# Summing the attention halves without GpSimd, and loading the spatial weights on the other queue

## The chip, the cores and the metric

The kernel runs on one core of a Trainium2 chip. The metric is the device time of one execution in microseconds; the time before is 2110.33 us, the median of three runs (2108.59 to 2112.67). The engines are named as the profile names them: PE is TensorE's matmul, PEld its weight load, ACT is ScalarE, DVE is VectorE, POOL is GpSimd, SP is SyncE. All work of an engine runs in the order in which it was emitted.

## The reference, cut to what matters

The program is a two-layer encoder block on a sequence of 1024 positions with 1024 features, in float32. Each layer is `x <- x + RMSNorm(mixer(RMSNorm(x)))`.

Layer 0 is a gated MLP. Three dense projections of width 2048 give u, v and g; v is normalised and mixed along each chunk of 128 positions by a 128x128 matrix per head (16 heads), then gated and projected back:

```python
u = gelu(u); v = layer_norm(gelu(v))
sg = einsum('hpq,bcqhd->bcphd', w_s, vc) + b_s
y = u * sg * silu(g);  return y @ w_out
```

Layer 1 is attention in three groups with strides 1, 4 and 16 (half window 64 keys), 16 heads of 64 features in each group, with a relative-position bias read from a table. The three groups' outputs are merged by their softmax denominators, gated and projected back:

```python
logits = q @ k.T * dh**-0.5 + bias[rel * dilation]   # masked outside the window
p = exp(logits - max);  o = (p / den) @ v;  lse = max + log(den)
y = sum_g softmax(lse)_g * o_g;  return (y * silu(gate)) @ w_out
```

## The kernel before, in words

**Numbers in two parts.** Every matmul operand is split into a high part, which is rounded to TensorE's reduced float32 form, and a low part, which is the rest. A product of two such operands is computed as high times high, high times low and low times high. ACT writes the high part and DVE (sometimes POOL) subtracts to get the low part. A class `Pieces` does this for all dense weights: it loads pieces of 128x512 into three buffers on SP's queue (L149), ACT makes the high part (L165), DVE the low part (L167), and up to eight pieces lie ready ahead of the matmuls.

**A written-out order.** There is no automatic scheduling. A `Plan` keeps a clock that each matmul advances by its modelled time, and a heap of steps with due times. After each dense matmul it emits the steps that have come due. So a due time is a place in the order of emission; an engine reaches the step when what it got before is done. `plan.until` emits further steps until a condition on the order holds.

**Layer 0.** First v for all 2048 columns is projected and kept in `gv`. Twelve transfers `toep_fill` (L477) write the bias rows of each group 128 times over into three tensors in HBM, four heads at a time: 768 KB for group 0, 1536 KB for group 1, 512 KB for group 2. They are due 20, 50, 80, ... 350 plan units after the first part of the v projection, on SP's queue, and the results are read only in layer 1. Then 16 heads follow: `dense` computes u and g of a head, two halves of 512 positions each, in two alternating PSUM banks "D", which ACT evacuates with gelu and silu. After each head `spatial` sets the steps of its mixing among the matmuls of the next head, from `t0`, half a unit after the end of the head's projections: `ws_load` (the head's 128x128 matrix `wsr` and its bias `bsr`, 64 KB each, on SP's queue), `ws_tr` (PE transposes the matrix, ACT and DVE split it), `v_split`, `ws_sum` and four times `mix`. `ws_load` is due at t0 - 6, which is past already when it is set, so it is emitted with the next matmul, just ahead of `ws_tr` at t0.

**Layer 1.** A unit is a pair of heads (p of 8) in one group (g of 3), 24 units in all. For each, `v_load` and `v_split` bring the values and split them into `u.vs`; `dense(q_part)` and `dense(k_part)` project queries and keys; their evacuation fills two tiles for queries and two for keys, one for each head of the pair (`a`). A key tile has two halves along its free axis: the first holds the high part on all 128 partitions (ACT writes 64, POOL copies them to the other 64, L932), the second holds the low part on 64 partitions (DVE) and zeros on the other 64 (POOL, L923). The tag "ks" has three buffers, a unit takes two. Then eight `attend` steps, four for each head of the pair, are laid over the following unit's projections: `qk` (PE into bank "S"), `smax` (DVE), `ex` (ACT), `trs` (PE transposes into bank "T"), `ph` and `pl` (ACT and DVE split the probabilities), `pv` (PE into bank "O"), and `o1`, `o2`, `o3`, which put the output together.

For `pv` the stationary operand is `u.vs` with 64 columns of high and 64 columns of low values, so 64 partitions of bank "O" hold products with the high values and 64 those with the low values; the moving operand holds high and low probabilities side by side, 256 columns for each of two blocks. In groups 0 and 2 all four products are summed: `o1` (ACT) copies 64 partitions x 512 columns from the other 64 partitions to `tm`, `o2` (DVE, L273) adds the own 64 partitions x 512 columns, and `o3` (POOL, L1087) adds the two column halves into `u.o`. In group 1 three products are computed and `o2` alone finishes.

When a pair's three groups are done, `weights` merges them in four quarters of 256 positions: the quarters 0 and 2 on POOL, 1 and 3 on DVE, for the last pair all on DVE. All other transfers of layer 1 (values through HBM, merge weights, results) are on SP's queue as well.

Of the kernel before, what the change touches and what calls it, by code (L numbers as in the profile page):

```python
# [203 lines left out]
def encoder_block(ctx: ExitStack, tc: tile.TileContext, x, norm_pre, norm_post, a_w_in, a_w_s,  # L204
# [269 lines left out]
    prep.close()  # L474

    def toep_fill(g, h):
        nc.sync.dma_start(toep[g][h:h + 4],  # L477
                            vec[h:h + 4, VOFF[g]:VOFF[g] + VLEN[g]].unsqueeze(1).to_broadcast(
                                [4, P, VLEN[g]]))

# [67 lines left out]
            pc.free(2)  # L548

    done_a = set()  # L550

    def spatial(h, ug, t0, dt):
        vs, sg, T = {}, {}, {}
        hc = slice(128 * h, 128 * h + 128)

        def ws_load():
            T["w"] = sp.tile([P, P], F32, name="wsr")
            nc.sync.dma_start(T["w"], a_w_s[h])
            T["b"] = sp.tile([P, P], F32, name="bsr")
            nc.sync.dma_start(T["b"], bcast_row(a_b_s, h * P, P))  # L560

        def ws_tr():
            b = bank("T")
# [34 lines left out]
            if cc == 3:  # L598
                done_a.add(h)

        plan.at(t0 - 6, ws_load)
        plan.at(t0, ws_tr)
        plan.at(t0 + 0.3, v_split, 0)
        plan.at(t0 + 1.5, v_split, 1)
        plan.at(t0 + 2.5, ws_sum)
        for cc in range(4):
            plan.at(t0 + 4.0 + dt * cc, mix, cc)

# [47 lines left out]
    for k in range(8):  # L656
        w_rows(b_w_out, 128 * k, 0)

    for h in range(NH):
        u = sp.tile([P, S], F32, name="us")  # L660
        g = sp.tile([P, S], F32, name="gs")
        dense(lambda b, hh: act(u[:, 512 * hh:512 * hh + 512], b, AF.Gelu_apprx_tanh))
        dense(lambda b, hh: act(g[:, 512 * hh:512 * hh + 512], b, AF.Silu))
        tt(u, u, g, OP.mult)
        if h == 0:
            plan.until(lambda: not any(f is ln_apply for _, _, f, _ in plan.heap))
        spatial(h, u, plan.now + 0.5, 3.0)
# [216 lines left out]
    def v_split(u, k):  # L884
        if k == 0:
            if u.prev is not None and u.prev.prev is not None:
                plan.until(lambda: u.prev.prev.pv_left == 0)
            u.vs = b1.tile([P, 8, 2, 2, 64], F32R, name="vs2")
        src = u.vt.rearrange("p m (a d) -> p m a d", a=2)
        hi = u.vs[:, :, :, 0, :]  # L890
        if k == 0:
            act(hi, src)
            plan.after(VALUES_AT[1], v_split, u, 1)
        else:
            tt(u.vs[:, :, :, 1, :], src, hi.bitcast(F32), OP.subtract)
            u.v_there = True

    def q_part(u):
        def evac(b, hh):
            if hh == 0:  # L900
                if u.prev is not None:
                    plan.until(lambda: u.prev.qk_left[0] == 0)
                plan.until(lambda: u.v_there)
                u.q = [b1.tile([P, S], F32R, name="qs", bufs=3) for _ in range(2)]
            for a in range(2):
                r = 64 * a
                act(place(u, u.q[a], r, r + 64, hh), source(u, b, r, r + 64), scale=-0.125)
            for a in range(2):
                r = 64 * a
                hi = place(u, u.q[a], r, r + 64, hh)  # L910
                stt(place(u, u.q[a], 64 - r, 128 - r, hh), source(u, b, r, r + 64), -0.125,
                    hi.bitcast(F32), OP.mult, OP.subtract)
        return evac

    def k_part(u):
        def evac(b, hh):
            if hh == 0:
                if u.prev is not None:
                    plan.until(lambda: u.prev.qk_left[0] == 0)
                u.k = [b1.tile([P, 2, S], F32R, name="ks", bufs=3) for _ in range(2)]  # L920
                for a in range(2):
                    o = 64 - 64 * a
                    nc.gpsimd.memset(u.k[a][o:o + 64, 1].bitcast(F32), 0.0)  # L923
            for a in range(2):
                r = 64 * a
                act(place(u, u.k[a][:, 0], r, r + 64, hh), source(u, b, r, r + 64))
# [23 lines left out]
    def attend(u, a, n, t0):  # L950
# [109 lines left out]
        def o1():  # L1060
            if u.o is None:
# [5 lines left out]
            w = 256 if g == 1 else 512  # L1067
            T["m"] = pool.tile([P, 512], F32, name="tm")
            act(T["m"][rs, :w], T["o"][64 - r0:128 - r0, :w])

        def o2():
            b, m = T["o"], T["m"]
            if g == 1:
                tt(res(u.o[rs]), b[rs, :256].rearrange("p (b j) -> p b j", b=2),
                   m[rs, :256].rearrange("p (b j) -> p b j", b=2), OP.add)
                u.o_left -= 1
            else:
                tt(m[rs], b[rs], m[rs], OP.add)

        def o3():  # L1080
            if g == 0:
                m = T["m"][rs].rearrange("p (i a b t) -> p a i t b", i=2, a=2, t=8)
# [373 lines left out]
```

## Time and profile before

| | before |
|---|---|
| median of three runs | 2110.33 us |
| profiled execution, whole | 2109.72 us |
| its span, first to last instruction | 2107.9 us |
| mean granted TensorE clock, share of full speed | 0.982 |
| PE busy | 2003.0 us (95%) |
| DVE busy | 1242.0 us (59%) |
| ACT busy | 1063.0 us (50%) |
| POOL busy | 413.5 us (20%) |

The span is 1.8 us shorter than the profiled execution, and that execution is 0.6 us below the median. On the span's axis the v projection ends at about 202 us, the 16 heads' projections run to about 622 us, the first output projection to about 833 us, the attention units from about 955 us, the last pair's from about 1822 us, and the second output projection ends the program. TensorE's clock has two levels, 1.2 and 2.4 GHz; the profile gives the granted clock of a stretch as a share of the higher one.

### The profile page before, as it was taken

How to read it: one execution, taken by the hardware profiler on the slowest of the kernel's cores; microseconds unless marked ns; L12 is line 12 of the kernel's file. 1: busy time of each engine (PE TensorE's matmuls, PEld its weight loads, DVE VectorE, ACT ScalarE, POOL GpSimd, SP SyncE). 2: the span in 40 equal slices, each digit the busy share in tenths (PEclk: the TensorE clock that was granted, in tenths of full speed). 3: DMA queues.
4: the chain of work that ended last, by engine and by line, in shares of the span. 5: the costliest groups of instructions: out<-in, count | busy, mean ns of one | idle time of the engine just before them, and what ended most of it. 6: DMA issues, size and time to landing. Idle time of an engine off the chain costs nothing.

```text
span 2107.9 us, 30338 instructions
## 1 busy us (share of the span) xinstructions
PE 2003.0 (95%) x10809; PEld 1709.1 (81%) x10809; DVE 1242.0 (59%) x2742; ACT 1063.0 (50%) x2239; POOL 413.5 (20%) x480
## 2 busy tenths in 40 slices
PE   7999898989999978999999999999999999999998
PEld 5888686868888757988888988888888889787776
DVE  6223443534456798346576575675765765767647
ACT  5222232323346676256655556556656555676632
POOL 1000000000000143012151250241331512525241
PEclk9999999999999999999999999999999999999999
DMA  4222121221113455331222241331322232413277
GB/s 148 82 84 68 65 80 65 79 66 56 55 35 121 153 172 186 124 89 54 81 84 86 76 114 52 93 99 56 101 72 82 82 87 75 109 46 85 92 208 272
DMA packets 222339, 201.97 MB, mean 96 GB/s; under 512 B 17179, under 2 KB 192955, under 8 KB 222188
## 3 DMA queue, kind: packets, MB, share of 16 engines
q1 hardware_dynamic: 222188, 200.04, 31.2%
q8 instruction: 85, 1.39, 0.3%
q14 instruction: 66, 0.54, 0.1%
HBM read 171.26 MB, written 40.26 MB: 100 GB/s over the span
## 4 chain that ended last, share of the span: by engine, by line
PE 75%; DVE 11%; DMA 6%; POOL 3%; issue 3%; ACT 2%; SPq 0%; DVEq 0%; ACTq 0%; POOLq 0%
PE psD L255 56%; PE psS L255 8%; PE psO L255 6%; PE psT L255 3%; DVE wt L167 3%; PE psT L266 3%; DMA wsr<-in_a_w_s_dram 3%; DVE o L273 1%; POOL o L1087 1%; DVE qs L276 1%; DVE tm L273 1%; POOL o L273 1%; DVE xs L1006 1%; DMA y<-yd 1%; ACT wt L165 1%
## 5 line engine op out<-in xcount | busy, mean ns | idle before, releaser
L255 PE MATMUL psD<-hTh,wt 128*128 128x512 f32 x2816 | 916.2, 398 | 0.0
L255 PEld LDWEIGHTS psD<-hTh,wt 128*128 128x128 f32 x2816 | 519.3, 190 | 90.3 <-ACT gv L270 0.4
L255 PE MATMUL psD<-hTl,wt 128*128 128x512 f32 x1408 | 559.2, 397 | 0.0
L255 PE MATMUL psD<-wt,hTh 128*128 128x256 f32 (+1 forms) x1760 | 365.4, 300 | 1.3 <-DMA gv<-in_x_dram 0.6
L167 DVE TENSOR_TENSOR wt<-raw,wt 128x512 fp32r<-128x512 f32 x344 | 268.8, 803 | 163.3 <-ACT wt L165 144.6
L255 PEld LDWEIGHTS psD<-hTl,wt 128*128 128x128 f32 x1408 | 267.6, 190 | 48.2
L255 PEld LDWEIGHTS psD<-wt,hTh 128*128 128x128 f32 x1760 | 286.4, 191 | 13.7 <-POOL wt L167 1.7
L165 ACT ACTIVATE wt<-raw 128x512 fp32r<-128x512 f32 x360 | 215.5, 626 | 157.7 <-PE psD L255 104.0
L255 PE MATMUL psD<-wt,hTl 128*128 128x256 f32 (+1 forms) x880 | 263.0, 299 | 0.7 <-DVE hTl L273 0.7
L270 ACT ACTIVATE xs<-xs,st 128x256 f32<-128x256 f32 (+2 forms) x384 | 176.8, 461 | 164.3 <-DVE st L1006 163.5
L1087 POOL TENSOR_TENSOR o<-tm 64x256 f32<-64x256 f32 x128 | 127.3, 995 | 385.1 <-DVE tm L273 375.3
L255 PEld LDWEIGHTS psD<-wt,hTl 128*128 128x128 f32 x880 | 168.3, 191 | 5.8 <-DVE hTl L273 1.3
L273 DVE TENSOR_TENSOR pt<-psT,pt 128x512 fp32r<-128x512 f32 (+1 forms) x192 | 115.1, 600 | 96.4 <-ACT pt L270 94.6
L273 POOL TENSOR_TENSOR yo<-yo,gp 128x1024 f32<-128x1024 f32 x6 | 15.8, 2628 | 725.2 <-ACT yo L270 719.2
L1006 DVE CUSTOM_DVE_ANT_0 xs<-psS,bias 128x256 f32<-128x256 f32 (+1 forms) x256 | 95.9, 412 | 76.5 <-PE psS L255 74.6
L255 PEld LDWEIGHTS psO<-pt,vs 128*128 128x128 f32 (+1 forms) x640 | 99.5, 178 | 32.3 <-DVE pt L273 18.6
L255 PE MATMUL psS<-ks,qs 128*128 128x256 f32 x640 | 111.8, 289 | 11.6 <-POOL ks L932 11.6
L255 PE MATMUL psO<-pt,vs 128*128 128x256 f32 (+1 forms) x640 | 108.5, 283 | 13.6 <-DVE pt L273 13.6
L273 DVE TENSOR_TENSOR ks<-psD,ks 64x512 fp32r<-64x512 f32 x96 | 66.1, 688 | 88.2 <-ACT ks L270 86.9
L255 PEld LDWEIGHTS psS<-ks,qs 128*128 128x128 f32 x640 | 98.2, 192 | 22.6 <-POOL ks L932 13.5
L932 POOL TENSOR_SCALAR ks<-ks 64x512 fp32r<-64x512 f32 x96 | 61.7, 642 | 279.4 <-ACT ks L270 273.7
L270 ACT ACTIVATE tm<-psO 64x512 f32<-64x512 f32 (+1 forms) x192 | 100.1, 521 | 31.8 <-PE psO L255 20.4
(204 smaller groups left out, 2742.9 us busy)
## 6 DMA issues: line engine op xcount, KB each, us to landing
raw<-in_b_w_in_dram SPq DMA_DIRECT2D x160, 256.0 KB, 3.2
raw<-in_a_w_in_dram SPq DMA_DIRECT2D x96, 256.0 KB, 3.0
raw<-in_a_w_out_dram SPq DMA_DIRECT2D x96, 256.0 KB, 2.8
y<-yd SPq DMA_DIRECT2D x56, 256.0 KB, 5.8
cb<-sc SPq DMA_DIRECT2D x64, 192.0 KB, 5.2
vd<-tm SPq DMA_DIRECT2D x80, 128.0 KB, 1.8
vt<-vd SPq DMA_DIRECT2D x16, 512.0 KB, 4.8
yd<-cb SPq DMA_DIRECT2D x28, 256.0 KB, 2.5
```

The lines of the kernel that those rows point to most:

```text
L165: self.nc.scalar.activation(hi, src, AF.Copy)
L167: e.tensor_tensor(lo, src, hi.bitcast(F32), op=OP.subtract)
L255: nc.tensor.matmul(o, l, r, start=start, stop=stop)
L266: nc.tensor.transpose(o, i, ident)
L270: nc.scalar.activation(o, i, f, **k)
L273: (e or nc.vector).tensor_tensor(o, a, b, op=op)
L276: nc.vector.scalar_tensor_tensor(o, a, s, b, op0=op0, op1=op1)
L932: nc.gpsimd.tensor_scalar(place(u, u.k[a][:, 0], o, o + 64, hh), hi.bitcast(F32), 1.0, 0.0, op0=OP.mult, op1=OP.add)
L1006: nc.vector.tensor_tensor_reduce(out=o, in0=s_, in1=bi, op0=OP.add, op1=OP.min, scale=1.0, scalar=3.0e38, accum_out=col(0, t))
L1087: nc.gpsimd.tensor_tensor(o, m[:, 0], m[:, 1], op=OP.add)
```

## The change: what it does

Three things are changed. `toep_fill` and `ws_load` issue their transfers from ACT's queue instead of SP's, and `ws_load` runs earlier: heads 0 and 1 are loaded before the loop over the heads, and head h + 2 is loaded four units after the `t0` of head h (the two tiles have two buffers each). The zeros of the first key tile are set when the unit's queries are evacuated instead of its keys; those of the second stay. In groups 0 and 2 the values of the second head of a pair are stored low first, so that the partitions on which the output lies always hold the products with the high values; the output is then the sum of three products instead of four (low times low is left out): `o1` copies 256 columns instead of 512, and `o2` and `o3` are two additions on DVE of 256 columns each, both with one operand in PSUM. POOL has no part in it any more.

```diff
     def toep_fill(g, h):
-        nc.sync.dma_start(toep[g][h:h + 4],
+        nc.scalar.dma_start(toep[g][h:h + 4],
...
+    def ws_load(h):
+
+        if h < NH:
+            T = ws[h] = {}
+            T["w"] = sp.tile([P, P], F32, name="wsr")
+            nc.scalar.dma_start(T["w"], a_w_s[h])
+            T["b"] = sp.tile([P, P], F32, name="bsr")
+            nc.scalar.dma_start(T["b"], bcast_row(a_b_s, h * P, P))
...
-        plan.at(t0 - 6, ws_load)
         plan.at(t0, ws_tr)
...
+        plan.at(t0 + 4.0, ws_load, h + 2)
...
+    ws_load(0)
+    ws_load(1)
     for h in range(NH):
...
-        hi = u.vs[:, :, :, 0, :]
+        v4 = u.vs.rearrange("p m a e d -> p m (a e) d")
+        hi, lo = (v4[:, :, 0:4:2], v4[:, :, 1:4:2]) if u.g == 1 else (v4[:, :, 0:4:3], v4[:, :, 1:3])
...
+    def k_tile(a):
+
+        t = b1.tile([P, 2, S], F32R, name="ks", bufs=3)
+        nc.gpsimd.memset(t[64 - 64 * a:128 - 64 * a, 1].bitcast(F32), 0.0)
+        return t
...
                 u.q = [b1.tile([P, S], F32R, name="qs", bufs=3) for _ in range(2)]
+                u.k = [k_tile(0)]
...
-                u.k = [b1.tile([P, 2, S], F32R, name="ks", bufs=3) for _ in range(2)]
-                for a in range(2):
-                    o = 64 - 64 * a
-                    nc.gpsimd.memset(u.k[a][o:o + 64, 1].bitcast(F32), 0.0)
+                u.k.append(k_tile(1))
...
-            act(T["m"][rs, :w], T["o"][64 - r0:128 - r0, :w])
+            T["m"] = pool.tile([P, 512], F32, name="tm")[:, :256]
+            src = T["o"][64 - r0:128 - r0]
+            if g == 1:
+                act(T["m"][rs], src[:, :256])
+            else:
+                act(T["m"][rs].rearrange("p (i q) -> p i q", i=2),
+                    src.rearrange("p (i e q) -> p e i q", i=2, e=2)[:, 0])
...
-                tt(m[rs], b[rs], m[rs], OP.add)
+                m = m[rs].rearrange("p (i q) -> p i q", i=2)
+                tt(m, b[rs].rearrange("p (i e q) -> p e i q", i=2, e=2)[:, 0], m, OP.add)
...
-                m = T["m"][rs].rearrange("p (i a q) -> p a i q", i=2, a=2)
+                m = T["m"][rs].rearrange("p (i q) -> p i q", i=2)
+                b = T["o"][rs].rearrange("p (i e q) -> p e i q", i=2, e=2)[:, 1]
                 o = u.o[rs, 256 * n:256 * n + 256].rearrange("p (i q) -> p i q", i=2)
-            nc.gpsimd.tensor_tensor(o, m[:, 0], m[:, 1], op=OP.add)
+            tt(o, b, m, OP.add)
```

## Rows read from the trace of the kernel before

**Rows 1.** The page's first part: busy us, share of the span, instructions.
```profile
PE 2003.0 (95%) x10809; PEld 1709.1 (81%) x10809; DVE 1242.0 (59%) x2742; ACT 1063.0 (50%) x2239; POOL 413.5 (20%) x480
```

**Rows 2.** Windows: PE, PEld, DVE, ACT, POOL busy; granted clock; DMA; units 1 to 6.
```profile
955.00:1822.00 867.00, 846.51 (x5203) 750.57 (x5202) 554.87 (x1331) 521.80 (x1239) 247.55 (x320) 1.00 0.29 82
```

**Rows 3.** What PE waited for in the heads (200 to 640): us, times, longest.
```profile
PE psT L266 <- DMA wsr<-in_a_w_s_dram: 29.0, 3, 10.4
```

**Rows 4.** SP's transfers in time, second of three such places: start, us.
```profile
323.61 0.61 SPq L477 DMA_DIRECT2D toep<-vec  x1
324.27 6.61 SPq L558 DMA_DIRECT2D wsr<-in_a_w_s_dram  x1
```

**Rows 5.** The chain of waits at that place: start, us.
```profile
324.27 17.74 DMA wsr<-in_a_w_s_dram
```

**Rows 6.** Windows right behind the three waits, columns as in rows 2.
```profile
235.00:246.00 11.00, 11.00 (x47) 9.17 (x48) 6.30 (x12) 4.14 (x6) 0.00 (x0) 0.86 0.17 49
342.00:353.00 11.00, 10.95 (x42) 9.04 (x43) 5.33 (x10) 4.14 (x6) 0.00 (x0) 0.76 0.17 48
450.00:461.00 11.00, 10.88 (x46) 9.07 (x47) 6.22 (x12) 4.14 (x6) 0.00 (x0) 0.86 0.17 49
```

**Rows 7.** Waits of ACT in the heads, and of SP's queue over the span.
```profile
ACT us L270 <- PE psD L255: 128.2, 32, 5.8
...
SPq L149 <- DVE wt L167: 1129.1, 219, 18.0
```

**Rows 8.** Groups by form: count | busy us, mean ns | idle before.
```profile
L1087 POOL TENSOR_TENSOR o<-tm 64x256 f32<-64x256 f32 x128 | 127.3, 995 | 385.1 <-DVE tm L273 375.3 <-PE psD L255 8.1
L273 DVE TENSOR_TENSOR tm<-psO,tm 64x512 f32<-64x512 f32 x128 | 87.8, 686 | 29.9 <-ACT tm L270 28.5
L270 ACT ACTIVATE tm<-psO 64x512 f32<-64x512 f32 x128 | 75.9, 593 | 17.5 <-PE psO L255 7.9 <-POOL o L1087 4.4 <-DMA vd<-tm 0.9
L923 POOL MEMSET ks<- 64x1024 f32 x48 | 45.6, 949 | 67.4 <-PE psS L255 66.1
L273 DVE TENSOR_TENSOR o<-psO,tm 64x256 f32<-64x256 f32 x64 | 26.8, 419 | 4.0 <-ACT tm L270 3.1
L270 ACT ACTIVATE tm<-psO 64x256 f32<-64x256 f32 x64 | 24.2, 378 | 14.2 <-PE psO L255 12.6 <-ACT pt L270 0.7
```

**Rows 9.** PE's waits in 955 to 1822 (two rows) and in 1822 to 2108.
```profile
PE psO L255 <- DVE pt L273: 11.6, 9, 2.4
PE psS L255 <- POOL ks L932: 8.9, 5, 2.9
...
PE psS L255 <- POOL ks L932: 2.7, 2, 1.6
```

**Rows 10.** Timeline of DVE, POOL and PE where group 0 hands over to 1.
```profile
1397.19 1.41 DVE L273 TENSOR_TENSOR ks<-psD,ks 64x512 fp32r<-64x512 f32 x2
1397.82 1.09 POOL L1087 TENSOR_TENSOR o<-tm 64x256 f32<-64x256 f32 x1
1399.00 1.96 POOL L932 TENSOR_SCALAR ks<-ks 64x512 fp32r<-64x512 f32 x2
1400.00 0.74 PE L255 MATMUL psS<-ks,qs 128*128 128x256 f32 x4 [2.90 <-POOL ks L932]
...
1688.54 1.41 DVE L273 TENSOR_TENSOR ks<-psD,ks 64x512 fp32r<-64x512 f32 x2
1689.04 0.86 PE L255 MATMUL psS<-ks,qs 128*128 128x256 f32 x4 [1.85 <-POOL ks L932]
```

**Rows 11.** Timeline of DVE, POOL and PE a little earlier in group 0, and a window.
```profile
1236.23 3.67 DVE L167 TENSOR_TENSOR wt<-raw,wt 128x512 fp32r<-128x512 f32 x2
1236.39 1.51 POOL L1087 TENSOR_TENSOR o<-tm 64x256 f32<-64x256 f32 x1 [4.58 <-DVE tm L273]
1240.56 0.74 PE L255 MATMUL psO<-pt,vs 128*128 128x256 f32 x4 [1.90 <-DVE pt L273]
1241.00:1246.00 5.00, 5.00 (x20) 4.02 (x19) 3.65 (x8) 3.23 (x8) 3.83 (x5) 0.66 0.54 150
```

More of the change, by code (lines that the diff above doesn't have):

```diff
@@ L550, in encoder_block @@
     done_a = set()
+    ws = {}
+    def ws_load(h):
[5 more added lines that the diff above has]
+            nc.scalar.dma_start(T["b"], bcast_row(a_b_s, h * P, P))
     def spatial(h, ug, t0, dt):
-        vs, sg, T = {}, {}, {}
+        vs, sg, T = {}, {}, ws.pop(h)
         hc = slice(128 * h, 128 * h + 128)
[L556 to L560, printed above, removed]
         def ws_tr():
@@ L894, in v_split @@
         else:
-            tt(u.vs[:, :, :, 1, :], src, hi.bitcast(F32), OP.subtract)
+            tt(lo, src, hi.bitcast(F32), OP.subtract)
             u.v_there = True
+    def k_tile(a):
+        t = b1.tile([P, 2, S], F32R, name="ks", bufs=3)
+        nc.gpsimd.memset(t[64 - 64 * a:128 - 64 * a, 1].bitcast(F32), 0.0)
+        return t
     def q_part(u):
@@ L1066, in o1 @@
                 u.o = pool.tile([P, S], F32, name=f"o{g}", bufs=2 if g == 0 else 1)
-            w = 256 if g == 1 else 512
-            T["m"] = pool.tile([P, 512], F32, name="tm")
-            act(T["m"][rs, :w], T["o"][64 - r0:128 - r0, :w])
+            T["m"] = pool.tile([P, 512], F32, name="tm")[:, :256]
[5 more added lines that the diff above has]
+                    src.rearrange("p (i e q) -> p e i q", i=2, e=2)[:, 0])
         def o2():
@@ L1074, in o2 @@
                 tt(res(u.o[rs]), b[rs, :256].rearrange("p (b j) -> p b j", b=2),
-                   m[rs, :256].rearrange("p (b j) -> p b j", b=2), OP.add)
+                   m[rs].rearrange("p (b j) -> p b j", b=2), OP.add)
                 u.o_left -= 1
             else:
-                tt(m[rs], b[rs], m[rs], OP.add)
+                m = m[rs].rearrange("p (i q) -> p i q", i=2)
+                tt(m, b[rs].rearrange("p (i e q) -> p e i q", i=2, e=2)[:, 0], m, OP.add)
         def o3():
             if g == 0:
-                m = T["m"][rs].rearrange("p (i a b t) -> p a i t b", i=2, a=2, t=8)
+                m = T["m"][rs].rearrange("p (i b t) -> p i t b", i=2, t=8)
+                b = T["o"][rs].rearrange("p (i e b t) -> p e i t b", i=2, e=2, t=8)[:, 1]
                 o = u.o.rearrange("p (t j b) -> p j t b", t=8, j=8)[rs, 2 * n:2 * n + 2]
             else:
-                m = T["m"][rs].rearrange("p (i a q) -> p a i q", i=2, a=2)
+                m = T["m"][rs].rearrange("p (i q) -> p i q", i=2)
+                b = T["o"][rs].rearrange("p (i e q) -> p e i q", i=2, e=2)[:, 1]
                 o = u.o[rs, 256 * n:256 * n + 256].rearrange("p (i q) -> p i q", i=2)
-            nc.gpsimd.tensor_tensor(o, m[:, 0], m[:, 1], op=OP.add)
+            tt(o, b, m, OP.add)
             u.o_left -= 1
```

## The prediction

> **What bounds the kernel now.** I read the busy shares first: PE is busy for 2003 of 2108 us [rows 1], so nothing gains that doesn't shorten a wait of PE or a stretch at the lower clock; all PE waiting together is 105 us. Then I looked at where PE waits, by what ends the wait. In the 16 heads of layer 0 nearly all of it is one thing: three times PE stands for about 10 us in front of the transpose of a spatial matrix until that matrix has landed, 29.0 us together [rows 3]. The queue's own rows say why: the matrix is issued 0.66 us behind a bias fill on the same queue [rows 4], and it lands 17.74 us later [rows 5], where a load without a fill ahead has landed before PE needs it (13 of 16 heads show no such wait). After each of these waits the granted clock is below full for a while: 0.86, 0.76 and 0.86 over the next 11 us [rows 6], a part of that time being spent at 1.2 instead of 2.4 GHz. In the attention units PE is busy for 846.5 of 867 us [rows 2]; the 20.5 us that are left are two waits: 8.9 us for POOL's copy of the keys and 11.6 us for DVE's low probabilities [rows 9]. Attention is thus close to PE's pace, with DVE (64% busy) and POOL (29%) late only in places.
>
> **Fills and spatial matrices.** Removed: the load directly behind the fill. Head h + 2 is now loaded while head h is mixed, about 1.8 heads or some 40 us ahead of its transpose, and heads 0 and 1 are loaded a whole projection ahead. A fill delays it by about 18 us [rows 4, 5], so the matrix is there in each case. That gives back the 29.0 us of waiting [rows 3]. What the lower clock took goes too: (1 - 0.86) x 11 = 1.5, (1 - 0.76) x 11 = 2.6 and 1.5 us, 5.7 us together [rows 6]. Sum 34.7 us. Is anything late next at that place? The dense weights: their loads on SP stood 1129 us waiting for a free buffer [rows 7], so they run far ahead of PE, and a fill that now shares the DMA engines with them instead of standing between them leaves them that lead. I count no loss.
>
> What the move costs: 12 fills and 32 small loads are issued by ACT, between its evacuations. SP's issue of a fill took 0.61 us [rows 4]; 44 x 0.6 = 26 us on ACT spread over some 530 us. ACT's evacuations of u waited 128.2 us in 32 waits for PE, 4.0 us each [rows 7]: this covers an issue. A load can hold its queue longer: right behind the fill SP was held 6.61 us [rows 4]. On ACT the next load comes about 10 us behind each 1536 KB fill in the heads (the due times: fills at 140, 230 and 320, heads ending at 145, 236 and 326 and the load 4.5 units later), when by that row the queue has room again. The new load also waits until DVE has read the bias of head h, in `ws_sum` 1.5 units earlier; behind it on ACT stand weight splits and the next evacuation, again under the 4.0 us. Bounds: 0 to 2.6 us for each of the three large fills (6.61 less 4.0), 0 to 8 us; I take 0, by the distance of 10 us.
>
> **The sum of the output.** Per step of groups 0 and 2 (16 of 24 units, 128 steps): POOL loses one instruction of 995 ns, 127 us in all; ACT's copy goes from 593 to 378 ns, the row of the same copy in group 1; DVE's addition of 686 ns becomes two of 419 ns, again the row of group 1 [rows 8]. DVE gets 838 - 686 = 152 ns more, 19.5 us in all; ACT gets 27.5 us back.
> The Trainium skill (VectorE: DVE Perf Modes, section on the TRN2 errata) speaks against this edit: it states a fixed cost for every instruction, 120 cycles with a PSUM source, and advises operands of 512 elements or more. By its figures one addition of 512 is 658 ns and two of 256 are 783 ns, so the extra would be 16.0 us by an estimate from that page; the rows' sum of 19.5 us is what I use.
> How much of the 19.5 us lies on the path? At most all (PE waiting for DVE throughout); but PE waits for DVE for 11.6 us in 867 us [rows 9], so most of it falls into DVE's own waiting, 28.5 us of which is `o2` waiting for ACT's copy [rows 8], which gets shorter by 0.215 us each time. Against it stands that POOL's addition and DVE's get in each other's way: two weight subtractions of DVE took 3.67 us beside POOL's additions (the group's mean is 0.80 each), and PE then waited 1.90 us for DVE [rows 11]. One such collision less is worth up to 1 us to DVE at just those places. So the wait for low probabilities has bounds from -11.6 (all gone) to +19.5 us; I take 0, the added instructions against the collisions, because both sit in the same stretches where DVE has no gap.
> A bank "O" is now held until the second addition. It is due 13.0 units into a step, and the `pv` that needs the bank is due 10.5 plus two spacings; the smallest spacing is 2.75 (22.0 / 8), so 3.0 units of slack against the longest wait for DVE of 2.4 us [rows 9]: nothing.
>
> **The keys' wait.** When group 0 hands over to group 1, POOL is busy without a gap: merge steps, key copies, both zero fills and three output additions, of which the last stands right in front of the key copy that PE waits for (1.09 us [rows 10]). Without the three additions of about 1.1 us and with one zero fill of 949 ns [rows 8] earlier, in POOL's idle time, the copy is ready some 4 us earlier, more than the longest wait of 2.9 us [rows 9]. What is late next is DVE's low part of the same keys: at 1400 its first half ends near 1397.9 and PE stood from 1397.1, so 2.1 of 2.9 us go, less 0.46 us for three longer sums on DVE: 1.6. At 1689 that half ends at 1689.2, after PE's start [rows 10]: nothing goes. By the same look at the others of the seven (1.5, 1.5 and 1.6 us whole, one nothing, the small last one half, 0.5), 6.7 of 11.6 us go. Bounds 0 and 11.6.
>
> **Sum.** 2109.7 (profiled execution, 1.8 us over its span) - 34.7 - 6.7 = 2068.3. The median is 0.6 us above the profiled execution: 2069 us.
>
> **Rivals.**
> A, attention gains more: POOL's disappearance also frees DVE. All waits for keys and probabilities go (11.6 + 11.6) and with them the lower clock behind them: 0.66 over 5 us, or 1.7 us, after the 1.90 us wait [rows 11], at some three such places, 5 us. For it: POOL's additions stand beside stretched DVE instructions [rows 11]. Against it: merge steps stay on POOL and collide as before. 2109.7 - 34.7 - 23.2 - 5 + 0.6 = 2047. The Trainium skill (SBUF — State Buffer, section on the two separate sides) would favour it: it describes the port that VectorE and GpSimd share as a lock, held for a whole instruction against VectorE instructions with two SBUF inputs, and the new additions have one input in PSUM.
> B, DVE becomes the bound where it is late already: the added 152 ns reach PE in the stretches without a gap, up to all 19.5 us, and the keys' wait only passes from POOL to DVE. For it: DVE is back to back around each hand-over. Against it: the shorter ACT copy. 2109.7 - 34.7 + 0.6 = 2075.6 with nothing, 2095 with all; about 2083.
> C, the other side: ACT is held for as long as the fill moves, because its queue takes nothing more, and PSUM isn't evacuated. It decides once ACT is held longer than its 4.0 us of waiting [rows 7]. Three fills of 1536 KB in the heads would cost 17.74 - 4.0 = 13.7 us each, 41 us, with the lower clock as now 5.7, two of half that size 4.9 each: 57 us. 2109.7 - 34.7 - 6.7 + 57 + 0.6 = 2126. For it: SP was held 6.61 us by the very next load; against it, the fill's own issue took 0.61 us [rows 4].
> D, the change doesn't do what it says: the matrices still come late because the fills now stand in front of them on ACT's queue. It would need 40 us of delay where 18 are seen [rows 5]. Then only the keys' 6.7 us: 2104.
>
> **How the numbers follow.** Forecast (2060 to 2075) 0.58, A 0.14, B 0.22, C 0.04, D 0.02. The range leaves out C, D, the far half of A and the far end of B: 2053 to 2085. A measurement tells about 0.2% (4 us) from no change; faster by more than that 0.95 (D with 2104 among it), within it 0.01, slower 0.04.
>
> **What would show it.** The wait of PE for `wsr` is gone and the granted clock of the heads is full; the stretch of the heads is 35 us shorter with the same matmuls. DVE has 128 instructions more and POOL 128 fewer; the group of 64x256 sums counts 320 at about 420 ns. The wait of PE for POOL's keys is under 5 us in all. I would be wrong if ACT shows long issues behind the fills (C), if PE's wait for DVE's low probabilities has grown by over 5 us (B), or if gelu evacuations end PE's waits in the heads.

## The result, and the profile after

The changed kernel takes 2047.75 us (median of 4 runs, 2044.72 to 2051.29), the kernel before beside it 2110.24 us: ratio 0.9704, 95% interval 0.9683 to 0.9724. The forecast was 2069 us with a range of 2053 to 2085; the time lies below it, where rival A (2047) had put it. The profiled execution took 2049.57 us, with a span of 2047.8 and a mean granted clock of 0.993 (before 0.982).

The page's first part, in the columns of [rows 1]:

```profile
PE 1988.7 (97%) x10809; PEld 1699.9 (83%) x10809; DVE 1235.6 (60%) x2870; ACT 1035.2 (51%) x2239; POOL 288.7 (14%) x352
```

The counts are as forecast: as many matmuls, DVE 128 instructions more, POOL 128 fewer. PE's busy time fell by 14.3 us with the same matmuls: more of them ran at the full clock. But DVE, which was to carry 19.5 us more, is busy 6.4 us less.

To see where 60 us of the span went I take three places that both chains of waits have: the last run of 43 matmuls in the heads, the run of 332 ahead of attention, and the first run of 22 behind it. The chain of before (start, us, what):

```profile
610.66 9.76 PE psD L255 x43
871.55 50.10 PE psD L255 x332
1865.54 5.04 PE psD L255 x22
```

The chain of after, the same three:

```profile
575.34 9.76 PE psD L255 x43
834.89 50.10 PE psD L255 x332
1809.01 5.03 PE psD L255 x22
```

The heads account for 35.1 us (610.66 - 575.34, less the 0.26 us by which they start earlier), the stretch up to attention for 1.3, the attention units for 19.9 (994.0 against 974.1), and what lies behind them, with the start, for 3.8. The last two, 5.1 us together, the forecast put at nothing.

Windows of after, columns as in [rows 2]: the heads, the attention units (the place of the window of [rows 2], with 28 matmuls more), and five microseconds in group 0 that answer to the window of [rows 11].

```profile
202.00:587.00 385.00, 384.72 (x1817) 321.18 (x1816) 186.19 (x350) 132.99 (x192) 0.00 (x0) 1.00 0.22 68
918.00:1771.00 853.00, 847.60 (x5231) 753.45 (x5230) 551.91 (x1431) 504.31 (x1246) 157.96 (x232) 1.00 0.30 84
1202.00:1207.00 5.00, 5.00 (x28) 4.18 (x27) 2.80 (x5) 2.54 (x5) 4.26 (x7) 1.00 0.61 151
```

In the heads PE now idles 0.28 us of 385, at the full 2.4 GHz; no row of [rows 3] is left. In the units 5.4 us of idleness remain of 20.5. And behind the place of [rows 11] the clock is 1.00 where it was 0.66: PE did not stop there.

What PE waited for in 918 to 1771, against [rows 9] (us, times, longest):

```profile
PE psO L255 <- DVE pt L273: 2.7, 4, 0.8
PE psS L255 <- DVE ks L273: 2.5, 3, 0.8
```

The keys' wait went from 8.9 us for POOL to 2.5 us for DVE, as expected. The wait for the low probabilities went from 11.6 to 2.7, and that was not expected.

A fill of 1536 KB on ACT's queue, and the load that follows it, against [rows 4]:

```profile
218.27 0.61 ACTq L477 DMA_DIRECT2D toep<-vec  x1
224.71 1.01 ACTq L558 DMA_DIRECT2D wsr<-in_a_w_s_dram  x1
```

The load comes 6.4 us behind this fill and holds ACT for 1.01 us; behind the other two fills of that size in the heads it comes 12.2 us later and takes 0.33. Only fills of 512 KB have a load directly behind them here; it holds ACT for up to 1.52 us. So nothing comes near the 4.0 us at which rival C begins. What a load directly behind 1536 KB would do to ACT, as it held SP for 6.61 us, this order never shows.

The groups by form, against [rows 8] (count | busy us, mean ns | idle before); the last line is that of DVE's weight subtractions, and the fence behind it shows the same line of before:

```profile
L273 DVE TENSOR_TENSOR tm<-psO,tm 64x256 f32<-64x256 f32 x128 | 53.6, 419 | 20.7 <-ACT tm L270 19.5
L273 DVE TENSOR_TENSOR o<-psO,tm 64x256 f32<-64x256 f32 x192 | 95.3, 496 | 7.3 <-ACT tm L270 3.1
L167 DVE TENSOR_TENSOR wt<-raw,wt 128x512 fp32r<-128x512 f32 x344 | 253.5, 759 | 161.3 <-ACT wt L165 142.9 <-PE psS L255 16.6
```

```profile
L167 DVE TENSOR_TENSOR wt<-raw,wt 128x512 fp32r<-128x512 f32 x344 | 268.8, 803 | 163.3 <-ACT wt L165 144.6 <-PE psS L255 16.7
```

The first sums cost 53.6 us, as the 419 ns of [rows 8] say. The second ones don't: 95.3 us less the 26.8 of group 1 is 68.5 us, or 535 ns each. Together 122.1 us in place of 87.8: DVE got 34.3 us of sums, not 19.5. The weight subtractions gave 15.3 of it back, DVE's merge steps (`o<-o,sgate`, `o<-o,cb`, `cb<-o,cb`, `o<-o`) 14.7, and the subtractions of 256 columns 6.2.

The place of [rows 11] shows how. POOL and DVE in before (start, us): the sum's addition of [rows 11] is followed at once by two merge steps, and DVE's two subtractions last from 1236.23 to 1239.9. Of these the first took 0.67 us; the addition, begun beside it, took 1.51; and the second subtraction took 3.08 and ended 0.55 us behind the second merge step.

```profile
1237.95 1.41 POOL L273 TENSOR_TENSOR o<-o,cb 128x256 f32<-128x256 f32 x2
1239.83 0.67 DVE L273 TENSOR_TENSOR pt<-psT,pt 128x512 fp32r<-128x512 f32 x1
```

The same place in after: the two subtractions take 1.28 us where they took 3.67, between two sums.

```profile
1197.16 0.41 DVE L273 TENSOR_TENSOR tm<-psO,tm 64x256 f32<-64x256 f32 x1
1197.49 1.28 DVE L167 TENSOR_TENSOR wt<-raw,wt 128x512 fp32r<-128x512 f32 x2
1198.69 0.65 DVE L273 TENSOR_TENSOR o<-psO,tm 64x256 f32<-64x256 f32 x1
1199.26 0.68 DVE L273 TENSOR_TENSOR pt<-psT,pt 128x512 fp32r<-128x512 f32 x1
```

Of the 118 subtractions in the units of before (955 to 1822) six, one per pair, fell under the addition and the merge steps behind it and took 2.47 us in the mean (up to 3.08); 82 met no POOL operation and took 0.69. Of the 118 in after (918 to 1771) 97 met none, 19 met a set or one merge step, and both kinds took 0.68 to 0.69 in the mean. There it is the merge step that takes longer, 1.00 us in place of 0.73, where it begins during a subtraction (1198.37).

### The profile page after: what moved, and what is told of

Its sections match the earlier page's. It is cut to its first block, busy times and chain, and to the rows that moved or that the text cites. A ratio compares the mean times of both kernels' runs of the same rounds, so it can differ in the third digit from the quotient of the medians.

```text
span 2047.8 us, 30244 instructions
## 1 busy us (share of the span) xinstructions
PE 1988.7 (97%) x10809; PEld 1699.9 (83%) x10809; DVE 1235.6 (60%) x2870; ACT 1035.2 (51%) x2239; POOL 288.7 (14%) x352
## 4 chain that ended last, share of the span: by engine, by line
PE 82%; DVE 9%; DMA 4%; ACT 2%; issue 2%; SPq 0%; DVEq 0%; ACTq 0%
PE psD L255 61%; PE psS L255 8%; PE psO L255 6%; PE psT L266 3%; PE psT L255 3%; DVE wt L167 2%; DVE o L273 1%; DMA cb<-sc 1%; DMA yd<-cb 1%; DVE rt L276 1%; DMA y<-yd 1%; DMA raw<-in_a_w_out_dram 0%; ACT wt L165 0%; DVE ks L273 0%; DVE pt L273 0%
## 5 line engine op out<-in xcount | busy, mean ns | idle before, releaser
L255 PEld LDWEIGHTS psD<-hTh,wt 128*128 128x128 f32 x2816 | 513.3, 188 | 88.9 <-ACT gv L270 0.4
L167 DVE TENSOR_TENSOR wt<-raw,wt 128x512 fp32r<-128x512 f32 x344 | 253.5, 759 | 161.3 <-ACT wt L165 142.9
L270 ACT ACTIVATE pt<-psT 128x512 fp32r<-128x512 f32 (+1 forms) x192 | 100.1, 521 | 27.2 <-PE psT L266 24.3
L266 PE MATMUL psT<-ident,xs 128*128 128x128 f32 x640 | 102.7, 273 | 4.2 <-ACT xs L270 3.6
```

The lines of the kernel that those rows point to most:

```text
L167: e.tensor_tensor(lo, src, hi.bitcast(F32), op=OP.subtract)
L255: nc.tensor.matmul(o, l, r, start=start, stop=stop)
L266: nc.tensor.transpose(o, i, ident)
L270: nc.scalar.activation(o, i, f, **k)
```

## The experiments

All ratios are to the kernel before, run beside them, with 95% intervals. "Units" is the time between the runs of 332 and of 22 matmuls: 994.0 us before, 974.1 after.

### The three parts, each alone

**loads_alone**: the kernel before with the fills and loads of after, `output_alone` with its values' order and sums, `zeros_alone` with its early zeros (the hunks of the diff shown ahead). In the cuts of code below `...` marks what is left out.

```diff
-        nc.sync.dma_start(toep[g][h:h + 4],
+        nc.scalar.dma_start(toep[g][h:h + 4],
...
+            nc.scalar.dma_start(T["w"], a_w_s[h])
...
-            nc.sync.dma_start(T["w"], a_w_s[h])
...
-        plan.at(t0 - 6, ws_load)
...
+        plan.at(t0 + 4.0, ws_load, h + 2)
```

> The kernel before with only the fills and the spatial loads on ACT's queue and the loads two heads ahead. All theories put 35 us on this part (the heads' stretch took 35.1 us less in the changed kernel): 2075 us, PE's wait for wsr gone, and in the attention units PE's waits as before (about 9 us for POOL's key copies, 11.6 us for DVE's low probabilities, three half-clock stretches). If the loads also free something for attention (a rival), it comes out at 2065 or less.

2069.3 us, 0.9812 (0.9795 to 0.9828), 6 us under the 2075 expected. The wait for `wsr` is gone, and the units are no shorter than before (996.9).

**output_alone**

```diff
...
-            nc.gpsimd.tensor_tensor(o, m[:, 0], m[:, 1], op=OP.add)
+            tt(o, b, m, OP.add)
```

> The kernel before with only the new summing of the outputs (values' order, o1, o2, o3; low times low left out). The first theory says that POOL's additions held up both DVE and POOL's own later steps: 20 to 25 us less, 2087 us, with PE's waits for low probabilities at 3 us and the half-clock stretches in attention gone. The rival that the zeros set early did it: under 8 us less, 2103 us.

2081.07 us, 0.9863 (0.9844 to 0.9881): the units fall to 972.6, by 21.4 us. All of the attention gain comes with this part.

**zeros_alone**

```diff
+                u.k = [k_tile(0)]
...
-                    nc.gpsimd.memset(u.k[a][o:o + 64, 1].bitcast(F32), 0.0)
+                u.k.append(k_tile(1))
```

> The kernel before with only the zeros of the first key tile set at the queries' evacuation. First theory: one zero fill of 0.95 us less in front of the key copies, 0 to 6 us less in all, 2107 us, the wait for low probabilities unchanged at 11 to 14 us. The rival that the zeros did it: 15 us less or more, 2095 us.

2107.46 us, 0.9991 (0.9976 to 1.0007): no difference that can be measured. What PE waited for in the units (us, times, longest):

```profile
PE psO L255 <- DVE pt L273: 13.4, 9, 2.2
PE psD L255 <- DVE ks L273: 1.1, 2, 0.9
PE psS L255 <- POOL ks L936: 1.1, 1, 1.1
```

The wait for POOL's keys shrinks from 8.9 to 1.1 us, but 11.6 us for DVE become 13.4 + 1.1, the clock falls at four places of the units instead of three (1.7 us each), and the units lose only 2.4 us: most of the wait only passes on.

The three parts alone give 41.0, 29.2 and 2.8 us, 73.0 in all, and together 62.5. In the profiled executions the units add up: 21.4 + 2.4 - 2.9 = 20.9 us against 19.9. The surplus lies outside them, between heads and attention (3.8 + 3.8 + 1.0 against 1.3) and behind attention (2.5 + 5.0 + 2.2 against 3.6), where none of the parts has an edit. So it is not a gain in attention that the parts share; why these two stretches vary by some us was not traced.

### Why the loads gain

**fills_on_act** moves the fills to ACT's queue and leaves the loads on SP and late.

```diff
-        nc.sync.dma_start(toep[g][h:h + 4],
+        nc.scalar.dma_start(toep[g][h:h + 4],
```

> The kernel before with only the fills on ACT's queue; the spatial loads stay on SP's queue at their old place just ahead of the transpose. If what held the matrix up was its place behind the fill in one queue, the stalls shrink to a few us: 2078 us. If the fill's traffic on the shared DMA engines held it, the three waits stay near 10 us each: 2105 to 2110 us.

2088.4 us, 0.9902 (0.9883 to 0.9921), at neither of the two times expected. PE in the heads:

```profile
PE psT L266 <- DMA wsr<-in_a_w_s_dram: 11.2, 2, 5.7
```

Of 29.0 us of waiting 11.2 stay, at two of the three places. One of them (start, us: the fill on ACT's queue, and the matrix's way from SP's queue until it has landed):

```profile
308.82 0.60 ACTq L477 DMA_DIRECT2D toep<-vec  x1
311.70 14.76 DMA wsr<-in_a_w_s_dram
```

The matrix lands 17.6 us behind the start of the fill, at the other place 17.5, though no fill stands ahead of it on its queue; in the kernel before it was 18.4 at both (for the first of them [rows 4, 5]). So it is the fill's traffic that holds the load, and the order on one queue is worth 0.8 to 0.9 us a place. The waits are shorter because the fills come at another time: at these two places PE needs the matrix 12.0 us behind the start of the fill instead of 9.1, and at the first place the fill comes 2.5 us behind the load, and PE does not wait. The Trainium skill (DMA: Bandwidth & Descriptors, Issuing engines are not separate DMA queues) says the same, that transfers from all issuing engines end up on the same 16 engines and interleave; this run agrees, with 17.6 us against 18.4.

**loads_ahead_on_sp** is `loads_alone` with everything left on SP.

> The kernel before with the spatial loads two heads ahead but everything still on SP's queue. If loading ahead alone is enough: PE's wait for wsr gone and 35 to 41 us less, 2070 to 2075. If the queue matters as well, because loads of weights now stand behind the fill and the matrices behind weights that wait for a buffer: waits of some us remain, 2080 or over.

2072.67 us, 0.9822 (0.9797 to 0.9848), no wait for `wsr`. Loading two heads ahead is enough; the other queue adds nothing that these intervals can tell from 0.9812. Directly behind a fill of 512 KB a load held SP for 1.88 us here (at 251.53), where ACT was held 1.46 in after.

### Why the sum gains: four parts of it put back

**copy_512_again**: after, with ACT's copy at 512 columns.

```diff
...
-                act(T["m"][rs].rearrange("p (i q) -> p i q", i=2),
-                    src.rearrange("p (i e q) -> p e i q", i=2, e=2)[:, 0])
+                act(T["w"][rs], src)
...
```

> The changed kernel with ACT copying 512 columns again (593 instead of 379 ns, 128 times, 27 us of ACT); the sums read the same 256 of them. First theory: 0 to 4 us more, 2048 to 2052. If ACT's shorter copy was what freed DVE: 10 us more or over, 2058 and up, with DVE's wait for ACT's copy back at 28 us.

2046.49 us, 0.9698 (0.9676 to 0.972), units 973.8: the shorter copy, which I had set against DVE's sums, is worth nothing that can be measured.

**dve_sums_doubled**: the first sum is done twice.

```diff
...
+                tt(T["w"][rs, 256:].rearrange("p (i q) -> p i q", i=2),
+                   b[rs].rearrange("p (i e q) -> p e i q", i=2, e=2)[:, 0], m, OP.add)
```

> The changed kernel with the first of the two sums on DVE done a second time into columns that nobody reads: 128 more instructions of 0.42 us, 54 us of DVE. It measures what a microsecond of DVE in these units costs. If the added sums are mostly hidden (as the changed kernel suggests, where DVE got 34 us of sums more): 5 to 15 us more, 2053 to 2063. If DVE is the bound: 40 us more or over.

2056.59 us, 0.9745 (0.9727 to 0.9762): 54 us more on DVE cost 8.8 (the two intervals leave 3 to 14), so about 0.16 us per us. DVE is not the bound (rival B).

**pool_adds_again**: POOL does an addition at the old place, its result unused.

```diff
...
+            nc.gpsimd.tensor_tensor(T["w"][rs, 256:], T["m"][rs], T["m"][rs], op=OP.add)
             tt(o, b, m, OP.add)
```

> The changed kernel, and POOL again adds 64x256 elements at each of the 128 steps, reading the copy in SBUF and writing columns that nobody reads. DVE's and ACT's own work is as in the changed kernel. If POOL's reading additions held up DVE (first theory): DVE's instructions with two SBUF inputs get longer again by some 20 to 40 us in sum, and the time goes up by 10 to 20 us, to 2060 to 2068. If only POOL's queue being late mattered: up by 3 to 8 us, 2051 to 2056, PE's wait for POOL's key copies back, the wait for low probabilities under 5 us. If ACT's shorter copy did it: no change.

2060.9 us, 0.9765 (0.9744 to 0.9787), units 985.4: 13 us of the gain go. That is the time that the first theory named, but its sign is missing: the subtractions' mean stays at 755 ns (759 in after). In the units 27 of 118 subtractions meet POOL's addition, nearly as many as before (30), but 20 of them still take 0.67 to 0.69 us and none more than 1.10; the addition itself takes 706 ns where it took 995, and no subtraction meets it together with merge steps. So this loss has another way. DVE and PE where group 0 hands over to group 1:

```profile
1205.60 0.78 DVE L273 TENSOR_TENSOR o<-o,cb 128x256 f32<-128x256 f32 x2 [4.70 <-DMA cb<-sc]
1210.49 0.74 PE L255 MATMUL psO<-pt,vs 128*128 128x256 f32 x4 [1.60 <-DVE pt L273]
```

DVE stands 4.70 us for the merge weights `cb` (2.18 in after), and then PE stands for DVE, 1.22 us at 1207.82 and 1.60 here. Over all hand-overs DVE's wait for `cb` is 21.0 us instead of 9.4. How POOL's work reaches this load is followed below, in `adds_apart`.

**pool_sets_instead**: two `memset` behind the second sum, which read nothing.

```diff
...
+            for _ in range(2):
+                nc.gpsimd.memset(T["w"][rs], 0.0)
```

> The changed kernel, and POOL sets the 64x512 copy to zero twice at each of the 128 steps, about 1 us of POOL that reads nothing from SBUF. First theory (reading additions hold up DVE): DVE's durations as in the changed kernel, and only the key copies may come late: 2048 to 2053. If POOL's time alone mattered: the same as with the additions again.

2082.2 us, 0.9867 (0.985 to 0.9884), units 1004.7. I had expected next to nothing, by the theory that only POOL's reads hurt. So that theory is not the whole: DVE's wait for `cb` is 35.4 us here.

### POOL's reads, and POOL's place in the order

**adds_apart** and **sets_apart** put POOL's work behind the second sum, with a target that nobody waits for: two additions that read `u.o` (`adds_apart`), or a tiny read and five `memset` (`sets_apart`).

```diff
+            for i in range(2):
+                d = ones[rs]
+                s = o[:, i]
...
+                nc.gpsimd.tensor_tensor(d, s, s, op=OP.add)
```

```diff
+            nc.gpsimd.tensor_tensor(ones[rs, 0:4], u.o[rs, 256 * n:256 * n + 4],
+                                    u.o[rs, 256 * n:256 * n + 4], op=OP.add)
+            for i in range(5):
+                nc.gpsimd.memset(ones[rs].bitcast(F32), 0.0)
```

> The changed kernel, and POOL adds twice 64x128 elements after each of the 128 second sums, reading the output row in SBUF that DVE has just written and writing a constant tile that nobody needs any more, so that no other engine waits for it except through POOL's own queue. If reading additions of POOL hold up DVE: DVE's instructions with two SBUF inputs get longer by 15 us or more in sum, and the time goes up by 8 to 20 us, 2056 to 2068. If POOL's queue alone matters: as much as with sets_apart.

> The changed kernel, and POOL reads four columns of the same row and then sets the constant tile to zero five times (64x128 each, about 1 us of POOL that reads nothing) after each of the 128 second sums. If only POOL's reads hold up DVE: 0 to 4 us more, 2048 to 2052. If POOL's queue being late for the key copies and the merge is what costs: 8 to 20 us more, 2056 to 2068, like adds_apart.

2084.47 us, 0.9887 (0.9867 to 0.9906), and 2076.76 us, 0.9854 (0.9834 to 0.9874), both above all that was expected; units 1005.0 and 1005.5. The longest of PE's waits from attention on, first with the additions, then with the sets:

```profile
PE psD L255 <- DVE ks L273: 17.3, 6, 3.1
```

```profile
PE psD L255 <- DVE ks L273: 12.0, 6, 3.0
```

Reading or not, 29 to 37 us more than after, by a new wait of up to 3.1 us, six times: PE needs a bank "D" that DVE frees when it has taken the keys from it. Behind it the clock is low (in `adds_apart` 0.50 from 1216 to 1222), which costs another 3.0 us by estimate, (1 - 0.50) x 6. No weight subtraction of the units meets an addition in `adds_apart`. Its first place can be followed back through the trace of `adds_apart` (start, us; DVE, POOL, SP's queue and PE):

```profile
1196.99 0.79 POOL L273 TENSOR_TENSOR cb<-o,cb 128x256 fp32r<-128x256 f32 x1
...
1206.16 1.23 SPq L1178 DMA_DIRECT2D cb<-sc  x2
1212.37 1.36 DVE L273 TENSOR_TENSOR o<-o,cb 128x256 f32<-128x256 f32 x2 [5.70 <-DMA cb<-sc]
1213.66 1.38 DVE L273 TENSOR_TENSOR ks<-psD,ks 64x512 fp32r<-64x512 f32 x2
1215.19 0.54 PE L255 MATMUL psD<-wt,hTh 128*128 128x256 f32 x2 [3.07 <-DVE ks L273]
```

The same steps in after:

```profile
1189.55 0.81 POOL L273 TENSOR_TENSOR cb<-o,cb 128x256 fp32r<-128x256 f32 x1
...
1198.69 1.23 SPq L1172 DMA_DIRECT2D cb<-sc  x2
1204.81 1.30 DVE L273 TENSOR_TENSOR o<-o,cb 128x256 f32<-128x256 f32 x2 [2.18 <-DMA cb<-sc]
1206.03 1.38 DVE L273 TENSOR_TENSOR ks<-psD,ks 64x512 fp32r<-64x512 f32 x2
```

This stretch runs 4.1 us later in `adds_apart` (its subtractions start at 1201.58 instead of 1197.49). Less these, POOL ends a merge quarter 3.3 us later, and its result leaves over SP's queue at once (1197.80). Behind it on that queue stand a load of `cb`, which needs the buffer that this frees (1200.28), DVE's own result, ready since 1198.50 (1201.98), and the load of the last quarter's `cb` (1206.16), 3.4 us later than in after. DVE, which stands at the merge step for that load, comes to the keys 3.5 us later: PE waits 3.07. So POOL's additions, queued between its merge steps, reach PE over transfers and over DVE's order. In `sets_apart` DVE stands 4.97 us for `cb` ahead of the same keys. There are two effects, then: POOL's reads, and POOL's place in the order.

**o3_on_dve**: the kernel before, with only POOL's addition given to DVE (two operands in SBUF, nothing else changed).

```diff
-            nc.gpsimd.tensor_tensor(o, m[:, 0], m[:, 1], op=OP.add)
+            tt(o, m[:, 0], m[:, 1], OP.add)
```

> The kernel before with one thing changed: its third step (the sum of the two column halves, both in SBUF) runs on DVE instead of POOL; ACT copies 512 columns and DVE adds 512 as before, the loads stay as before. DVE gets 128 x 0.42 to 0.65 us, 54 to 83 us, more. If POOL's absence is what gained, at the price of 0.16 us for a microsecond of DVE that the doubled sums showed: 21 less 9 to 13 plus 5, some 8 to 16 us faster than before, 2094 to 2102. If the shorter sums themselves gained: no faster than before, 2110 or over.

2095.08 us, 0.9932 (0.9907 to 0.9956), inside the forecast. What DVE gets:

```profile
L273 DVE TENSOR_TENSOR o<-tm 64x256 f32<-64x256 f32 x128 | 77.8, 608 | 3.4
```

77.8 us more for DVE, and still 14 us less in all (units 981.5): POOL's absence is worth more than a dear addition.

**before_sets** separates the reads from the order. It is the kernel before; POOL keeps its wait and its place, but writes zeros with two `memset` and reads nothing; the sums are left out of the output.

```diff
-            nc.gpsimd.tensor_tensor(o, m[:, 0], m[:, 1], op=OP.add)
+            nc.gpsimd.memset(T["m"][rs], 0.0)
+            nc.gpsimd.memset(o, 0.0)
```

> The kernel before with POOL's last addition of groups 0 and 2 replaced by two zero fills (the 64x512 copy and the 64x256 output), which wait for DVE's sum as the addition did and take about as long, but read nothing from SBUF; these sums are left out of the output. If POOL's reading additions held up DVE: at the one place per pair where a weight subtraction of DVE took 3.08 us beside POOL's addition and the merge behind it, it takes 0.7 to 1.7, the wait for low probabilities falls from 11.6 to under 6 us, and 6 to 14 us go, 2096 to 2104. If only POOL's order and lateness counted: unchanged within 3 us.

2090.04 us, 0.9906 (0.9881 to 0.993): 18 us gained, 14.1 of them in the units (979.9), and 4 more than the most that was expected. The place of [rows 11] in this run:

```profile
1232.82 1.28 DVE L167 TENSOR_TENSOR wt<-raw,wt 128x512 fp32r<-128x512 f32 x2
1232.95 0.52 POOL L1087 MEMSET tm<- 64x512 f32 x1 [4.76 <-DVE tm L273]
1233.42 0.30 POOL L1088 MEMSET o<- 64x256 f32 x1
1233.97 1.44 POOL L273 TENSOR_TENSOR o<-o,cb 128x256 f32<-128x256 f32 x2
1234.02 0.68 DVE L273 TENSOR_TENSOR pt<-psT,pt 128x512 fp32r<-128x512 f32 x1
```

The subtractions, the same two, run through in 1.28 us beside the sets, and the probabilities are split at 1234.02, before the merge steps matter. PE in the units, and the window behind this place:

```profile
PE psO L255 <- DVE pt L273: 5.6, 7, 1.0
PE psS L255 <- POOL ks L932: 3.6, 5, 0.8
PE psD L255 <- DVE ks L273: 2.4, 3, 1.3
```

```profile
1236.00:1241.00 5.00, 5.00 (x27) 4.20 (x26) 1.51 (x4) 3.62 (x8) 4.58 (x7) 1.00 0.62 177
```

Waits of 20.5 us become 11.6, and behind this place the clock stays full; of the three falls of the clock in the units the last is left. At this place it was the reading: POOL is as near, and DVE runs on. Of the 8.9 us of waiting that go, 6.0 are those for the low probabilities; the 2.9 for keys may also come from the sets being shorter than the addition (0.82 against 0.995 us). The Trainium skill (SBUF — State Buffer, SBUF: two separate sides) describes it: a VectorE instruction with two SBUF inputs and a GpSimd operation that reads SBUF exclude each other for a whole instruction. These rows agree: the subtraction, with both inputs in SBUF, was held, and `memset` does not hold it.

### What follows from it

**merge_on_dve** takes the merge steps from POOL too.

```diff
-            e = nc.vector if last or k % 2 else nc.gpsimd
+            e = nc.vector
```

> The changed kernel with all four quarters of the merge on DVE, so that POOL has only the key copies, the zeros and some weight pieces. DVE gets some 14 quarters of 3 us, about 42 us, more, at 0.16 us each 7 us; if POOL's remaining additions still hold up DVE and the key copies, 5 to 12 us come back: 2043 to 2050. If DVE is late at just that place already: 2055 to 2070.

2076.67 us, 0.9848 (0.9821 to 0.9874), 29 us worse than after and above both forecasts. PE from attention on:

```profile
PE psO L255 <- DVE pt L273: 23.1, 10, 4.1
```

DVE is now late with the split of the low probabilities, by up to 4.1 us. So the 0.16 us per us hold for sums spread over the steps and not for DVE's time as such; the merge steps are better left where they are.

**post_scale_on_dve** and **post_all_on_dve** look for the same collision elsewhere: behind the first output projection (587 to 798) POOL's additions and products stand beside DVE's subtractions. There ACT's scaling and POOL's gain become one instruction of DVE; the second kernel moves the residual sums to DVE too.

```diff
-                act(o, v, scale=T["r"])
-            else:
-                tt(o, o, g, OP.mult, nc.gpsimd)
+                stt(o, v, T["r"], g, OP.mult, OP.mult)
...
-            tt(y, y, T["x"], OP.add, nc.vector if fast else nc.gpsimd)
+            tt(y, y, T["x"], OP.add)
```

> The changed kernel; in the chain behind the first output projection the two scalings of a row (ACT by the root, POOL by the gain, 2.6 us each) are one instruction of DVE of about 1.28 us. There DVE's weight subtractions take 1.65 us where POOL is busy (21 times) and 0.68 where not. If POOL's reading operations hold up DVE there: 12 x 1.28 = 15 us more on DVE, 14 less from two thirds of the collisions, and a shorter chain: 2040 to 2050. If not: 2050 to 2060.

> As post_scale_on_dve, and the residual sums of that chain (POOL, 2.6 us each) run on DVE too, 6 x 1.22 = 7 us: no POOL operation that reads SBUF is left in the stretch. First theory: all 28 us of lengthened DVE instructions go for 23 us added, PE's 19 us of waiting there falls by a third, 2036 to 2046. Rival (DVE's time counts fully there): 2050 to 2060.

2034.35 us, 0.9646 (0.9625 to 0.9666), and 2029.88 us, 0.9619 (0.9596 to 0.9642). Both lie below what was expected; the second is 18 us below after, and their intervals overlap. The window 587 to 798, first after, then this one (columns as in [rows 2]):

```profile
587.00:798.00 211.00, 191.67 (x825) 153.02 (x824) 173.97 (x295) 142.97 (x227) 50.31 (x19) 0.96 0.48 153
```

```profile
587.00:798.00 211.00, 200.60 (x933) 163.54 (x932) 172.34 (x347) 139.66 (x234) 7.04 (x6) 0.98 0.51 169
```

DVE runs 52 instructions more in less time (172.34 us), and PE does 108 matmuls more in the same 211 us; PE's wait for DVE's weights in it falls from 15.6 to 9.3 us. The weight subtractions in this window, first after, then this kernel:

```profile
L167 DVE TENSOR_TENSOR wt<-raw,wt 128x512 fp32r<-128x512 f32 x95 | 84.3, 897 | 7.2 <-ACT wt L165 7.2
L167 DVE TENSOR_TENSOR wt<-raw,wt 128x512 fp32r<-128x512 f32 x97 | 67.0, 699 | 7.0 <-ACT wt L165 6.9
```

So the collisions are gone (784 ns in `post_scale_on_dve`). The chain of a row became shorter too, two steps of over 2 us being one of 1.28; how much of the gain is that, these runs don't separate.

## Why the prediction was right and wrong

**Fills and spatial matrices: right.** Forecast 34.7 us, measured 35.1 in the heads' stretch, with both halves of the term: no wait, and a full clock. The cause was right in that the load stood behind the fill; but it is the fill's traffic that holds it, on either queue (`fills_on_act`), and that the other queue adds nothing (`loads_ahead_on_sp`) I had left open by counting the move as one piece.

**The load on ACT: right.** 0 of bounds 0 to 8, and for the reason given: the loads came 6.4 to 12.2 us behind the large fills. The longest hold seen is 1.5 us.

**The keys' wait: right in sum, by luck, and wrong in what it gives by itself.** Forecast 6.7 of 11.6 us, measured 7.1 (11.6 to 4.5 over the span; in the units 8.9 to 2.5). But by place it came out otherwise: at 1400 1.3 us were to stay and 0.14 did, at 1689 all 1.85 and 0.12 did, while the three waits that were to go whole kept 0.82, 0.83 and 2.01. There PE now waits for DVE's low part of the keys, whose time I had read off the kernel before. And `zeros_alone` shows that without the freed DVE the wait is passed on to the low probabilities.

**The wait for low probabilities: the step that failed.** "So the wait for low probabilities has bounds from -11.6 (all gone) to +19.5 us; I take 0, the added instructions against the collisions". Measured: -8.9. Both sides of that balance were mis-sized. The collisions I priced at "up to 1 us" a piece; the one at the place of [rows 11] held DVE 2.4 us (3.67 against 1.28), and there is one per pair just ahead of a split that PE needs (the six held DVE 1.8 us in the mean, 2.47 less 0.69). I had compared it with the group's mean of 0.80 us and not with DVE's own lateness at that place. On the other side I let the added sums weigh fully where DVE "has no gap"; `dve_sums_doubled` prices them at about 0.16 us per us, so even the 34.3 us that they really took weigh some 5.5 us by that rate.

**The lower clock behind the waits: left out of the sum.** I had it, with 5 us, in rival A alone. There are three such stretches in the units of before, that of [rows 11] and these two windows:

```profile
1530.00:1536.00 6.00, 5.26 (x20) 4.27 (x21) 4.95 (x12) 3.29 (x8) 3.69 (x4) 0.72 0.51 145
1820.00:1826.00 6.00, 5.10 (x18) 4.11 (x19) 4.69 (x11) 3.29 (x8) 3.53 (x4) 0.72 0.58 146
```

(1 - 0.66) x 5 + 2 x (1 - 0.72) x 6 = 5.1 us. With the waits' 8.9 + 6.4 that is 20.4 us, where the chain says 19.9. So of the 18.7 us that the profiled execution gained beyond the forecast, 13.2 lie in the units, in the main in these two terms; 5.1 lie outside heads and attention, where nothing was forecast, and 0.4 in the heads.

**Rivals.** A came out in mechanism, and I gave it 0.14. That its 2047 is met within 1 us is partly luck: it took 28.2 us off attention, where 19.9 went; the 5.1 us outside heads and attention, and 2.3 by which the medians differ more than the profiled executions, make up the rest. My argument against it, that merge steps stay on POOL and collide as before, is what failed in it: by themselves they come too late to matter at this place (`before_sets`, 1233.97), and of the ten subtractions that meet merge steps in the units of after one is lengthened, to 1.22 us; they hurt behind an addition that has already held DVE back. B falls by `dve_sums_doubled`, C and D by the rows of ACT's queue and by the heads, C without its condition having arisen.

**Open.** Why the stretches ahead of and behind attention differ by some us between kernels that leave them alone, and how the 18 us of `before_sets` divide between the reads and the shorter time of POOL.

## What to carry to other kernels

Price a collision of two engines at its place, by what the delayed instruction does to the engine that waits for it and to the clock behind that wait, not by the group's mean. A load that must not be late behind a large transfer is issued earlier; another queue alone gave 0.8 to 0.9 us here. Work taken off an engine that reads the same memory can be worth more than the time that it adds elsewhere: look for the longest of a group, and for what overlaps it. When a part alone moves a wait to the next engine (`zeros_alone`), its gain belongs to the part that frees that engine.

## What the runs showed of the hardware

Three things I had not expected. An addition of 64x256 with one operand in PSUM took 0.419 us in the first sum and 0.43 in the second sum of group 2, and 0.59 to 0.68 us in the second sum of group 0, where operands and target are read and written in scattered order. Sets on POOL, which hold no subtraction of DVE (0.68 us beside them), can still cost 29 to 35 us by where they stand in POOL's order. And a wait of PE of 1.90 us was followed by five microseconds at a granted clock of 0.66 [rows 11], nearly as dear as the wait itself.
